# RMSNorm on one core: gamma on GpSimd's own queue, one early single-row store for three, and the last tile stored whole

## The chip, the cores and the metric

One core of a Trainium2 chip. The metric is the device time of one execution in microseconds (us); lower is better. The granted TensorE clock was 1.00, and TensorE has two instructions here, so the clock plays no part.

## The reference

```python
# x: 16 x 1024 x 512 float32, gamma: 512 float32 (all ones)
rms = np.sqrt(np.mean(x ** 2, axis=-1, keepdims=True) + 1e-5)
return (x / rms * gamma).astype(np.float32)
```

Input and output are 33.55 MB each, and nothing is reused between rows: 67.1 MB have to pass the DMA engines once.

## The kernel before

The 16384 rows are cut in 4 tiles of 128 partitions x 32 rows. Three slots of SBUF hold a tile each; tile 3 comes into slot 0 after tile 0 has been stored from it. A group is 16 rows of a tile (7 and 9 at the start). ScalarE squares, VectorE (DVE) sums, ScalarE takes the root and VectorE the reciprocal. Then GpSimd (POOL) takes `share` rows of the group through both multiplications; ScalarE scales the others one by one, and VectorE multiplies them by gamma in one instruction. All transfers are issued by SyncE (SP) in the order of the program.

```python
    pieces = (0, 128, 224, 320, 416, D)
    load(0, 0, 0, 1)                       # tile, slot, first row, end row
    load(0, 0, 1, 8)
    for c0, c1 in zip(pieces, pieces[1:]):
        nc.sync.dma_start(out=gamma_row[:, c0:c1], in_=gamma.unsqueeze(0)[:, c0:c1])
    load(0, 0, 8, 16)
    load(0, 0, 16, 32)
    load(1, 1, 0, 16)
    # ... ones_col, matmul gamma_psum = ones x gamma_row, later gamma_b = copy of gamma_psum
    groups = [                             # tile, first row, rows, pieces to square, GpSimd's share
        (0, 0, 7, (7,), 3), (0, 7, 9, (9,), 5), (0, 16, 16, (7, 9), 7),
        # ... (all with share 7)
        (3, 16, 16, (7, 5, 4), 3),
    ]
    # ...
    def transfers(t, g):                   # after the group's last instruction is written
        if (t, g) == (0, 0):
            store(0, 0, 0, 1)
            load(1, 1, 16, 32)
            store(0, 0, 1, 2)
            load(2, 2, 0, 23)
        elif (t, g) == (0, 16):
            store(0, 0, 2, 3)
            load(2, 2, 23, 32)             # these rows are scratch of the squares until then
            store(0, 0, 3, 16)
            store(0, 0, 16, 32)
            load(3, 0, 0, 16)
            load(3, 0, 16, 32)
        elif (t, g) == (1, 16):
            store(1, 1, 0, 32)
        elif (t, g) == (2, 16):
            store(2, 2, 0, 32)
        elif (t, g) == (3, 0):
            store(3, 0, 0, 16)
        elif (t, g) == (3, 16):
            store(3, 0, 16, 32)
    # ... for every group, with the squares of the next one in between:
        scale_by_pool(rstd, t, g, n, share)
        scale(rstd, t, g, 0, half)
        scale(rstd, t, g, half, mine)
        times_gamma(t, g, 0, mine)
        transfers(t, g)
```

## Time and profile before

| | before |
|---|---|
| median of the first three runs | 161.52 us (161.37 to 161.54) |
| the profiled execution | 161.95 us, span 160.2 us |
| DVE, ACT, POOL busy | 112.0, 107.8, 106.4 us |
| DMA share, first packet of x to last packet | 1.00 over 157.25 us |
| bytes moved | 67.12 MB in 2747 packets |

The prediction shows the lines that carry the bound. What the change moves at the start is seen in the timeline of SyncE's queue (start, us, issuer, line, transfer, count), kernel before:

```profile
0.74 0.86 SPq L45 DMA_DIRECT2D slot<-in_x_dram  x2
1.65 1.48 SPq L58 DMA_DIRECT2D gamma_row<-in_gamma_dram  x5
3.17 5.39 SPq L45 DMA_DIRECT2D slot<-in_x_dram  x3
27.35 0.35 SPq L49 DMA_DIRECT2D out_dram<-slot  x1
27.74 0.43 SPq L45 DMA_DIRECT2D slot<-in_x_dram  x1
28.27 0.38 SPq L49 DMA_DIRECT2D out_dram<-slot  x1
```

The times are those of the issue and not of the transfer: the single-row store issued at 27.35 ran at about 32, behind the 12.6 MB of loads issued before it.

### The profile page before, as it was taken

To read this page: it belongs to the slowest core of one execution; us is meant where nothing else is said; L and a number is where in the kernel's file an instruction comes from. 1 tells how busy PE (TensorE), PEld (TensorE's weight loads), DVE (VectorE), ACT (ScalarE), POOL (GpSimd) and SP (SyncE) were. 2 spreads that over 40 slices of the span, in tenths; PEclk is the share of its full clock that TensorE was granted. 3 is DMA by queue.
4 is the path that set the end of the run, shared out by engine and by line. 5 is a ranking of instruction groups with operands and counts; after the bars stand their busy time and mean duration, and the time that the engine had idled before them with its cause. 6 is when DMAs were issued, how large, how long until landed. Compare 5 with 4: busy or idle time off the path is not lost.

```text
span 160.2 us, 276 instructions
## 1 busy us (share of the span) xinstructions
PE 2.0 (1%) x2; PEld 0.5 (0%) x2; DVE 112.0 (70%) x39; ACT 107.8 (67%) x108; POOL 106.4 (66%) x24
## 2 busy tenths in 40 slices
PE   0050000000000000000000000000000000000000
PEld 0010000000000000000000000000000000000000
DVE  0018098899798999999999999999999009700000
ACT  3071967976999998999899899989960990000000
POOL 1000951994999599999999999999999980000000
DMA  5999999899999899999999999996996996999994
GB/s 189 431 421 475 442 401 458 340 446 491 417 435 494 388 379 383 426 450 475 434 401 426 483 401 393 524 491 295 524 491 295 524 491 295 401 491 417 401 450 196
DMA packets 2747, 67.12 MB, mean 419 GB/s; under 512 B 313, under 2 KB 314, under 8 KB 826
## 3 DMA queue, kind: packets, MB, share of 16 engines
q1 hardware_dynamic: 2746, 67.11, 98.1%
q14 instruction: 1, 0.01, 0.0%
HBM read 33.56 MB, written 33.55 MB: 419 GB/s over the span
## 4 chain that ended last, share of the span: by engine, by line
DVE 59%; ACT 22%; DMA 4%; ACTq 0%; issue 0%; SPq 0%
DVE ss L97 36%; DVE slot L122 23%; ACT slot L118 8%; ACT slot L96 7%; ACT sq_psum L96 6%; DMA slot<-in_x_dram 4%; DVE ss L103 1%; ACT ss L102 1%; ACTq L208 0%; ACT gamma_b L165 0%; SPq L45 0%; ACTq L96 0%
## 5 line engine op out<-in xcount | busy, mean ns | idle before, releaser
L109 POOL TENSOR_TENSOR slot<-slot,ss 128x3584 f32<-128x3584 f32 (+2 forms) x9 | 47.0, 5218 | 24.1 <-DVE ss L103 24.1
L110 POOL TENSOR_TENSOR slot<-slot,gamma_b 128x3584 f32<-128x3584 f32 (+2 forms) x9 | 59.3, 6587 | 0.7
L97 DVE TENSOR_REDUCE ss<-sq_psum 128x7 f32<-128x3584 f32 (+1 forms) x13 | 42.2, 3247 | 13.7 <-ACT sq_psum L96 13.7
L118 ACT ACTIVATE slot<-slot,ss 128x512 f32<-128x512 f32 x75 | 47.3, 706 | 4.7 <-DVE ss L103 4.7
L122 DVE TENSOR_TENSOR slot<-slot,gamma_psum 128x4608 f32<-128x4608 f32 (+2 forms) x9 | 41.3, 4590 | 8.7 <-ACT slot L118 8.7
L96 ACT ACTIVATE sq_psum<-slot 128x3584 f32<-128x3584 f32 (+1 forms) x13 | 34.6, 2658 | 6.4 <-DMA slot<-in_x_dram 5.7
L97 DVE TENSOR_REDUCE ss<-slot 128x9 f32<-128x4608 f32 x3 | 14.9, 4954 | 4.4 <-ACT slot L96 4.2
L97 DVE TENSOR_REDUCE ss<-sq_sbuf 128x5 f32<-128x2560 f32 x5 | 14.0, 2803 | 0.0
L96 ACT ACTIVATE slot<-slot 128x4608 f32<-128x4608 f32 x3 | 12.1, 4033 | 0.0
L96 ACT ACTIVATE sq_sbuf<-slot 128x2560 f32<-128x2560 f32 x5 | 11.6, 2321 | 0.0
L102 ACT ACTIVATE ss<-ss,eps_t 128x16 f32<-128x16 f32 (+2 forms) x9 | 2.7, 305 | 11.9 <-DVE ss L97 11.9
L103 DVE RECIPROCAL ss<-ss 128x16 f32<-128x16 f32 (+2 forms) x9 | 2.1, 236 | 0.4 <-ACT ss L102 0.4
L66 PE MATMUL gamma_psum<-gamma_row,ones_col 1*128 1x512 f32 x2 | 2.0, 1122 | 8.6 <-DMA gamma_row<-in_gamma_dram 8.6
L72 ACT ACT_TABLE_LOAD x1 | 1.3, 1283 | 1.2 <-PEq L197 1.2
L165 ACT COPY gamma_b<-gamma_psum 128x512 f32<-128x512 f32 x1 | 0.6, 567 | 0.0
L66 PEld LDWEIGHTS gamma_psum<-gamma_row,ones_col 1*128 1x128 f32 x2 | 0.5, 308 | 8.6 <-issue 8.6
L64 POOL MEMSET ones_col<- 1x128 f32 x1 | 0.2, 195 | 0.3 <-POOLq L197 0.3
L197 POOL MEMSET const-float32-0.0<- 128x1 f32 x1 | 0.1, 99 | 0.2 <-issue 0.2
L72 ACT ACTIVATE table<-eps_t 128x1 f32<-128x1 f32 x1 | 0.2, 202 | 0.0
L197 POOL MEMSET const-bfloat16-1.0<- 128x1 bf16 x1 | 0.1, 102 | 0.0
L197 POOL MEMSET const-uint8-127<- 128x1 uint8 x1 | 0.1, 102 | 0.0
L197 POOL MEMSET const-float32-1.0<- 128x1 f32 x1 | 0.1, 99 | 0.0
(1 smaller groups left out, 0.1 us busy)
## 6 DMA issues: line engine op xcount, KB each, us to landing
slot<-in_x_dram SPq DMA_DIRECT2D x5, 4096.0 KB, 21.9
out_dram<-slot SPq DMA_DIRECT2D x3, 4096.0 KB, 23.4
slot<-in_x_dram SPq DMA_DIRECT2D x1, 5888.0 KB
out_dram<-slot SPq DMA_DIRECT2D x1, 3328.0 KB, 21.8
slot<-in_x_dram SPq DMA_DIRECT2D x1, 2304.0 KB, 14.3
slot<-in_x_dram SPq DMA_DIRECT2D x1, 2048.0 KB, 9.9
slot<-in_x_dram SPq DMA_DIRECT2D x1, 1792.0 KB, 7.0
out_dram<-slot SPq DMA_DIRECT2D x3, 256.0 KB
```

The lines of the kernel that those rows point to most:

```text
L66: nc.tensor.matmul(gamma_psum[:, 0], ones_col, gamma_row, start=True, stop=True)
L72: nc.scalar.activation(out=table, in_=eps_t, func=AF.Sqrt)
L96: nc.scalar.activation(out=sq[:, :m], in_=rows, func=AF.Square)
L97: nc.vector.tensor_reduce(out=ss[:, r : r + m, 0], in_=sq[:, :m], axis=mybir.AxisListType.X, op=OP.add)
L102: nc.scalar.activation(out=ss[:, :n, 0], in_=ss[:, :n, 0], func=AF.Sqrt, bias=eps_t, scale=1.0 / D)
L103: nc.vector.reciprocal(out=ss[:, :n, 0], in_=ss[:, :n, 0])
L109: nc.gpsimd.tensor_tensor(out=part, in0=part, in1=by_row, op=OP.mult)
L110: last = nc.gpsimd.tensor_tensor(out=part, in0=part, in1=gamma_b.to_broadcast([P, share, D]), op=OP.mult)
L118: nc.scalar.activation(out=x[:, g + r, :], in_=x[:, g + r, :], func=AF.Copy, scale=rstd[:, r])
L122: scaled = nc.vector.tensor_tensor(out=part, in0=part, in1=gamma_psum.to_broadcast([P, r1 - r0, D]), op=OP.mult)
L165: nc.scalar.copy(out=gamma_b[:, 0], in_=gamma_psum[:, 0])
L197: nc = _bacc.Bacc("TRN2", target_bir_lowering=False, num_devices=1)
```

## The change

The intent is fewer transfers: gamma as one transfer on another queue, two single-row stores fewer, and one store for tile 3 in place of two. Since the last store then waits for the last group, the compute of that group is shortened: GpSimd takes 5 rows for 3, and VectorE starts after the first half of the scaling.

```diff
-    for c0, c1 in zip(pieces, pieces[1:]):
-        nc.sync.dma_start(out=gamma_row[:, c0:c1], in_=gamma.unsqueeze(0)[:, c0:c1])
+    nc.gpsimd.dma_start(out=gamma_row, in_=gamma.unsqueeze(0))
...
-        (3, 16, 16, (7, 5, 4), 3),
+        (3, 16, 16, (7, 5, 4), 5),
...
             load(1, 1, 16, 32)
-            store(0, 0, 1, 2)
             load(2, 2, 0, 23)
         elif (t, g) == (0, 16):
-            store(0, 0, 2, 3)
             load(2, 2, 23, 32)
-            store(0, 0, 3, 16)
+            store(0, 0, 1, 16)
...
-        elif (t, g) == (3, 0):
-            store(3, 0, 0, 16)
         elif (t, g) == (3, 16):
-            store(3, 0, 16, 32)
+            store(3, 0, 0, 32)
...
         scale(rstd, t, g, 0, half)
+        if not ahead:
+            times_gamma(t, g, 0, half)
...
-        times_gamma(t, g, 0, mine)
+        times_gamma(t, g, 0 if ahead else half, mine)
```

More of the change, by code (lines that the diff above doesn't have):

```diff
@@ L52 @@
     gamma_row = const.tile([1, D], fp32)
-    pieces = (0, 128, 224, 320, 416, D)
     load(0, 0, 0, 1)
     load(0, 0, 1, 8)
-    for c0, c1 in zip(pieces, pieces[1:]):
-        nc.sync.dma_start(out=gamma_row[:, c0:c1], in_=gamma.unsqueeze(0)[:, c0:c1])
+    nc.gpsimd.dma_start(out=gamma_row, in_=gamma.unsqueeze(0))
     load(0, 0, 8, 16)
```

## The prediction

> **What bounds the kernel now.** I began with the page's busy shares and the strips of 40 slices. No compute engine is over 70%, but the DMA strip is at 9 nearly from end to end:
>
> ```profile
> PE 2.0 (1%) x2; PEld 0.5 (0%) x2; DVE 112.0 (70%) x39; ACT 107.8 (67%) x108; POOL 106.4 (66%) x24
> ...
> DMA  5999999899999899999999999996996996999994
> ...
> DMA packets 2747, 67.12 MB, mean 419 GB/s; under 512 B 313, under 2 KB 314, under 8 KB 826
> ```
>
> The 6s near the end look like holes, so I asked the windows view for three stretches: before the first data packet, the stream, and after its last packet. I chose the borders from the packet records of the trace (first packet of x at 1.75 us, last one ends at 158.99). The columns are the stretch, its length, five engines' busy time, the granted clock, the DMA share and GB/s:
>
> ```profile
> 0.00:1.75 1.75, 0.00 (x0) 0.00 (x0) 0.00 (x0) 0.60 (x1) 0.44 (x6) 1.00 0.02 1
> 1.75:159.00 157.25, 2.04 (x2) 0.50 (x2) 112.05 (x39) 107.25 (x108) 106.00 (x18) 1.00 1.00 427
> 159.00:160.17 1.17, 0.00 (x0) 0.00 (x0) 0.00 (x0) 0.00 (x0) 0.00 (x0) 1.00 0.00 0
> ```
>
> The share is 1.00 over the whole 157.25 us, and this settles it: the 16 DMA engines never wait for work. The 6s come from counting long packets in the slice in which they start (one 64 KB packet takes 2.42 us in the records, more than half a slice). The span is 1.75 us of start, 157.25 us of transfer and 1.17 us of end.
>
> The chain that ended last gives DVE 59% and the DMA 4%, which would say that DVE is the bound. Its last piece shows what it leaves out: it follows instructions, and the last instruction ends at 139.14 us, 21 us before the span does.
>
> ```profile
> 132.05 7.09 DVE slot L122
> ```
>
> What follows that piece is seen in the SyncE queue's waits, where L208 is the end of the program (us in total, times, longest), and in the timeline of the last group:
>
> ```profile
> SPq L208 <- DMA out_dram<-slot: 19.6, 3, 9.6
> ```
>
> ```profile
> 123.95 8.07 ACT L118 ACTIVATE slot<-slot,ss 128x512 f32<-128x512 f32 x13 [4.72 <-DVE ss L103]
> 125.56 2.75 POOL L109 TENSOR_TENSOR slot<-slot,ss 128x1536 f32<-128x1536 f32 x1
> 125.62 13.91 SPq L49 DMA_DIRECT2D out_dram<-slot  x2
> 128.38 3.43 POOL L110 TENSOR_TENSOR slot<-slot,gamma_b 128x1536 f32<-128x1536 f32 x1
> 132.05 7.09 DVE L122 TENSOR_TENSOR slot<-slot,gamma_psum 128x6656 f32<-128x6656 f32 x1 [8.13 <-ACT slot L118]
> ```
>
> The first half of tile 3 is issued for storing at 125.62 and the second at about 139.2. By the packet records tile 2's store holds the engines until 138.7 (the first engine free) to 139.6 (the last), the first half of tile 3 until about 149, the second until 158.99. The second half was thus issued nearly 10 us before an engine could start on it. Compute ends early enough, and its time is hidden.
>
> **What the Trainium skill says.** "DMA: Bandwidth & Descriptors", section "Where 436 GB/s comes from", gives 435.2 GB/s as the ceiling of the ports. The trace agrees: 427 GB/s on average, 437 between 102 and 138 us (a window that rounds at packets), and 27.1 bytes per ns in a 64 KB packet, times 16 engines 434. So there is no unused bandwidth, beyond some 2 us of small and slow packets. The same page, "Issuing engines are not separate DMA queues", says that transfers issued by SyncE, ScalarE or GpSimd run on the same 16 engines, and that another issuer saves issue time only. The kernel before issues all from one queue (q1) and can't test it; the change can. "Why a DMA increments its semaphore by 16 and not by 1" says that one increment comes from each engine that a transfer uses. The trace agrees: 19 large transfers x 16, plus five gamma pieces with one data packet and one increment each, of which four have data under 512 B, are 304 + 5 + 4 = 313, the page's count under 512 B. "Latency and other measured facts" puts the first byte at about 0.6 us for SyncE's path and about 1 us for GpSimd's. Here the first load is issued at 0.74 (0.38 us of issue) and its packets start at 1.75; GpSimd's path is in no run yet.
>
> **The change part by part.**
>
> *Gamma.* Five issues (1.48 us of SyncE's time from 1.65 us on) leave SyncE's queue, so the next load is issued some 1.5 us sooner. That buys nothing: it was issued at 3.17, and its first packets run at 7.2, behind the 2 MB ahead of it. The five packets take 22 to 27 ns, with their increments about 0.16 us, on whichever engine holds them. On GpSimd's queue the built program cuts the row in 16 pieces of 128 B: one small packet and one increment on each engine, about 0.03 us each. The matmul that waits for gamma (8.6 us) should go sooner, but its first readers are the copy of gamma at 15.63 and GpSimd's multiply at 18.87. GpSimd's two memsets get later by the time of one issue; ScalarE is idle until 8.31 for x, so this is hidden. Worth: 0 to -0.15 us.
>
> *Early stores.* Rows 1 and 2 of tile 0 lose their own stores and go with the 13-row one, which becomes 15 rows. Bytes are equal, packets fewer: two transfers x 8 packets on each engine. A 2 KB packet takes 84 ns, where 27.1 bytes per ns would make 75.6: about 8 ns are fixed. The large ones agree: two 32 KB packets (1213 ns each) against one of 64 KB (2418) differ by 8 ns. So 16 x 8.4 = -0.13 us, and two increments of 9 ns, -0.02. The loads of tiles 1 and 2 come 0.7 to 1.4 us sooner in the queue, and the first rows' store later; nobody waits for either. The load of rows 23 to 31 of tile 2 still waits for DVE until 49.8, while the queue has work until about 56 (57.3 before, less two single-row stores of 0.7).
>
> *Tile 3 whole.* 8 packets and one increment fewer on each engine: -0.07 and -0.01 us. The store now waits for the last group. GpSimd takes 5 rows in place of 3: from 125.56 on, by the 5-row instructions already in this kernel (4.46 and 5.61 us, with gaps 10.14), it ends at 135.7. ScalarE scales 11 rows at 8.07 / 13 = 0.62 us: six are done at 127.7, all at 130.8. DVE multiplies them in two goes, at 0.54 us a row plus 0.1 (from 9 rows in 4.94 and 13 in 7.09): 6 rows to 131.0, 5 rows to 133.8. So GpSimd is last, the store is issued at 135.75, and with the 1.0 us that the first load needed its packets can run from 136.8. The first engine is free at 138.7 less the 0.2 saved so far: 138.5. Margin 1.7 us, so no hole.
>
> *Sum:* -0.13 - 0.02 - 0.07 - 0.01 - (0 to 0.15) = -0.23 to -0.38 us of 157.25. I take -0.3: 161.52 - 0.3 = 161.2.
>
> **Rivals.**
>
> *Compute was the bound after all.* The chain's shares speak for it, and the last instruction ends 3.4 us sooner (139.14 to 135.7): the time would be 158.1, just over 2% faster. The DMA share of 1.00 speaks against it.
>
> *The queue runs dry before the last store.* Tile 3's first half no longer fills the time while the last group is computed. If GpSimd or DVE ended 3 us later than I reckon, near 139 as before, the packets would start at 140.2: a hole of some 1.7 us, and 162.9. The durations of these instructions repeat to within 1% through the trace (seven-row multiplies 7.78 to 7.81), so I give it little. It is why the change moves two rows to GpSimd and splits DVE's work: without these two the whole store would lose time.
>
> *Slow packets.* Against the usual duration of their size, packets lose about 1.4 us per engine in all, in four places: the first 4 us, and the ends of the loads at 29 to 31, 61.5 to 62.5 and 99 us, each with a long run of stores (or the first row's) next in the queue. These three switches stay; the two that go (at 42 and 57 us) show no loss. So I expect no gain, but this is the widest uncertainty: half a microsecond either way.
>
> *GpSimd's queue costs something at start or end*, such as preparing descriptors before the first instruction, or one more queue to close. No view of before shows it. It could add 0.3 to 1 us outside the stream.
>
> **Range and chances.** The argument rests on the stream's 1.00 share, so all terms are tenths of a microsecond, and 2% is 3.2 us. The three runs of before lie within 0.17 us. Slow packets and the new queue set the range: 160.6 to 161.9. Faster by over 2% needs the first rival, slower needs the second twice as bad as reckoned: 2% each.
>
> **What would show it.** DMA share 1.00 from the first packet to the last; about 2340 packets (14 x 128 large, 2 x 128 of 2 KB, 16 x 16 increments, 32 for gamma) with the same bytes; GpSimd's last instruction ending at 135.7, DVE's near 133.8; the last store issued just after; the waiting at the program's end some 24 us on one store. The chain of waits should end 3.4 us earlier with the span hardly changed. I am wrong if the share dips between 135 and 141 us, if the stream starts later than 1.8 us, if the end takes more than 1.2 us after the last packet, or if packets of one size take other times than before.

## The result, and the profile after

Changed: median 161.51 us (161.43 to 161.68, 6 runs). Before, in the same rounds: 161.46 us (161.33 to 161.54, 6 runs). Ratio 1.0005, 95% interval 0.9992 to 1.0018, so the same. A ratio here is the mean time of one kernel's runs over that of the other's of the same rounds, so not quite the ratio of the medians. Executions over 1.5% slower than the fastest of the same kernel are left out of the means. 161.51 lies in the range of 160.6 to 161.9, but the forecast gain of 0.3 us isn't there: 0.3 us would be a ratio of 0.998, outside the interval.

The page of the changed kernel, the DMA strip, the packets, the queues and the shares of the chain that ended last:

```profile
DMA  6999999899998899999999999996996997999974
...
DMA packets 2337, 67.12 MB, mean 420 GB/s; under 512 B 288, under 2 KB 288, under 8 KB 544
...
q1 hardware_dynamic: 2304, 67.11, 98.1%
...
q0 software_dynamic: 32, 0.00, 0.0%
...
POOL 46%; ACT 18%; DVE 12%; DMA 4%; POOLq 4%; issue 0%; SPq 0%; ACTq 0%
```

The packets are those reckoned (2337, predicted about 2340), and gamma is on a queue of its own with 32. The chain has turned from DVE (59%) to POOL (46%) without any effect on the time: it names whichever engine ended its instructions last, and the DMA ends some 23 us after it. SyncE's waiting for stores at the program's end is 22.5 us in two waits, the longest 19.3, where some 24 us on one store were predicted.

The windows view of the changed kernel (stretch, length, five engines, clock, DMA share, GB/s), cut at its own last packet:

```profile
0.00:1.75 1.75, 0.00 (x0) 0.00 (x0) 0.00 (x0) 0.60 (x1) 0.73 (x5) 1.00 0.00 0
1.75:158.50 156.75, 2.04 (x2) 0.49 (x2) 111.05 (x40) 106.01 (x106) 110.25 (x21) 1.00 1.00 428
158.50:159.70 1.20, 0.00 (x0) 0.00 (x0) 0.00 (x0) 0.00 (x0) 0.00 (x0) 1.00 0.00 0
```

The start is the same, the end a little longer (1.24 us after the last packet at 158.47, 1.17 before; more than 1.2 was one of the prediction's signs of being wrong), and the share is 1.00 again. The stream is 0.5 us shorter than in the trace of before (156.75 for 157.25). On two traces alone one would say that the change saved 0.5 us. The timed runs deny it, because the profiled execution of before was a long one; the first experiment shows this.

The last group in the timeline of the changed kernel, engine by engine:

```profile
123.89 6.85 ACT L116 ACTIVATE slot<-slot,ss 128x512 f32<-128x512 f32 x11 [4.72 <-DVE ss L101]
...
125.47 4.47 POOL L107 TENSOR_TENSOR slot<-slot,ss 128x2560 f32<-128x2560 f32 x1
130.02 5.61 POOL L108 TENSOR_TENSOR slot<-slot,gamma_b 128x2560 f32<-128x2560 f32 x1
...
127.71 6.08 DVE L120 TENSOR_TENSOR slot<-slot,gamma_psum 128x3072 f32<-128x3072 f32 x2 [3.85 <-ACT slot L116]
...
135.65 0.33 SPq L49 DMA_DIRECT2D out_dram<-slot  x1
```

GpSimd ends at 135.63 (predicted 135.7), VectorE at 133.79 (133.8), the store is issued at 135.65 (135.75). By the packet records the first engine is free for it at 138.63 (138.5).

Gamma, from the timeline of GpSimd and the waits (in all, times, longest) of the changed kernel:

```profile
1.22 0.67 POOL L56 DMA_DIRECT2D gamma_row<-in_gamma_dram  x1 [0.78 <-POOLq L193]
```

```profile
PE gamma_psum L64 <- DMA gamma_row<-in_gamma_dram: 7.2, 1, 7.2
```

The matmul goes at 7.2 in place of 8.6 us and nobody gains by it: its readers come at 15.6 and 18.8. It is only 1.4 us sooner because gamma's packets first run at 5.47, 4.3 us after the issue began.

### The profile page after: what moved, and what is told of

The parts are those of the page before. It is cut to its first block, busy times and chain, and to the rows that moved or that the text cites. A ratio compares the mean times of both kernels' runs of the same rounds, so it can differ in the third digit from the quotient of the medians.

```text
span 159.7 us, 264 instructions
## 1 busy us (share of the span) xinstructions
PE 2.0 (1%) x2; PEld 0.5 (0%) x2; DVE 111.0 (70%) x40; ACT 106.6 (67%) x106; POOL 111.0 (69%) x25
## 2 busy tenths in 40 slices
DMA packets 2337, 67.12 MB, mean 420 GB/s; under 512 B 288, under 2 KB 288, under 8 KB 544
## 4 chain that ended last, share of the span: by engine, by line
POOL 46%; ACT 18%; DVE 12%; DMA 4%; POOLq 4%; issue 0%; SPq 0%; ACTq 0%
POOL slot L108 24%; POOL slot L107 22%; DVE ss L95 9%; ACT slot L94 7%; ACT sq_psum L94 6%; DMA slot<-in_x_dram 4%; POOLq L204 4%; ACT slot L116 3%; DVE slot L120 3%; ACT ss L100 1%; ACT gamma_b L159 0%; SPq L45 0%; DVE ss L101 0%; POOLq L107 0%; ACTq L94 0%
## 5 line engine op out<-in xcount | busy, mean ns | idle before, releaser
L107 POOL TENSOR_TENSOR slot<-slot,ss 128x3584 f32<-128x3584 f32 (+2 forms) x9 | 48.7, 5407 | 22.9 <-DVE ss L101 22.9
L108 POOL TENSOR_TENSOR slot<-slot,gamma_b 128x3584 f32<-128x3584 f32 (+2 forms) x9 | 61.5, 6828 | 0.7
L116 ACT ACTIVATE slot<-slot,ss 128x512 f32<-128x512 f32 x73 | 46.0, 706 | 4.7 <-DVE ss L101 4.7
L120 DVE TENSOR_TENSOR slot<-slot,gamma_psum 128x4608 f32<-128x4608 f32 (+3 forms) x10 | 40.3, 4040 | 4.4 <-ACT slot L116 4.4
L56 POOL DMA_DIRECT2D gamma_row<-in_gamma_dram x1 | 0.7, 667 | 0.8 <-POOLq L193 0.8
```

The source lines that it names most:

```text
L56: nc.gpsimd.dma_start(out=gamma_row, in_=gamma.unsqueeze(0))
L107: nc.gpsimd.tensor_tensor(out=part, in0=part, in1=by_row, op=OP.mult)
L108: last = nc.gpsimd.tensor_tensor(out=part, in0=part, in1=gamma_b.to_broadcast([P, share, D]), op=OP.mult)
L116: nc.scalar.activation(out=x[:, g + r, :], in_=x[:, g + r, :], func=AF.Copy, scale=rstd[:, r])
L120: scaled = nc.vector.tensor_tensor(out=part, in0=part, in1=gamma_psum.to_broadcast([P, r1 - r0, D]), op=OP.mult)
```

## The experiments

The runs were made in four batches, each on one chip with the kernel before beside it. "Slow packets" is worked out from the packet records: the duration of each packet over the usual one of its size (1213 ns for 32 KB, 686 for 18 KB), where the excess is more than 15 ns, summed over a stretch and divided by 16 engines. "Landing" is the last store's completion: each transfer increments its semaphore once per engine, so the trace has 16 times for it, and I give the median and the last. "Tail" is the span less the last landing, and "waits" are the wait instructions with which SyncE, at the end of the program, still has to go through other semaphores at or after that landing. The median is of the timed runs; all columns from "slow packets" on are of the one execution that was profiled, whose own time stands beside the median and is up to 1.2 us longer.

| kernel | median us | profiled us | slow packets 28 to 32.5 us | 32.5 to 65 | 97 to 104 | landing, median | landing, last | SyncE's transfers | waits | tail |
|---|---|---|---|---|---|---|---|---|---|---|
| before, the first trace | 161.52 | 161.95 | 0.27 | 0.39 | 0.22 | 158.85 | 159.34 | 24 | 1 | 0.83 |
| before again | 161.56 | 161.48 | 0.25 | 0.26 | 0.07 | 158.65 | 158.87 | 24 | 1 | 0.83 |
| changed | 161.51 | 161.48 | 0.27 | 0.38 | 0.08 | 158.63 | 158.81 | 16 | 1 | 0.90 |
| changed again | 161.62 | 161.61 | 0.18 | 0.52 | 0.07 | 158.59 | 158.94 | 16 | 1 | 0.90 |
| gamma only | 161.95 | 163.17 | 0.36 | 0.25 | 0.09 | 158.67 | 160.20 | 19 | 6 | 1.20 |
| early stores only | 161.77 | 161.77 | 0.27 | 0.44 | 0.09 | 158.82 | 159.04 | 22 | 3 | 0.96 |
| tile 3 whole only | 162.07 | 162.29 | 0.41 | 0.22 | 0.31 | 158.91 | 159.62 | 23 | 2 | 0.89 |
| whole store, compute as before | 162.56 | 162.51 | 0.12 | 0.71 | 0.03 | 159.74 | 159.83 | 16 | 1 | 0.90 |
| 14 more transfers | 162.62 | 163.68 | 0.56 | 0.10 | 0.63 | 159.81 | 160.88 | 30 | 3 | 1.02 |
| 29 more transfers | 166.39 | 165.67 | 0.17 | 0.50 | 1.12 | 161.26 | 162.81 | 45 | 4 | 1.09 |
| gamma and early stores | 161.82 | 162.05 | 0.19 | 0.70 | 0.19 | 159.00 | 159.21 | 17 | 4 | 1.06 |
| no early store | 161.84 | 161.75 | 0.00 | 0.90 | 0.04 | 158.86 | 159.02 | 15 | 2 | 0.96 |
| rows between loads | 161.85 | 161.77 | 0.28 | 0.25 | 0.10 | 158.60 | 158.88 | 18 | 5 | 1.11 |
| rows before loads | 162.50 | 162.47 | 0.88 | 0.02 | 0.05 | 159.12 | 159.57 | 18 | 5 | 1.12 |

### The kernel before, against itself

No edit.

> The kernel before, against itself, as the floor of noise and for a second trace. The trace that the prediction was made from took 161.95 us, 0.43 more than the median of the timed runs (161.52), so its stream of 157.25 us may have been an outlier. If it was, this run's span is near 159.8 us in place of 160.2 and the DMA stream (first packet of x to last packet) near 156.8 us; then the change saved nothing in the stream. If the stream is 157.2 us again while the time is 161.5, the stream is not what the timed runs lose. Ratio 1.000 with an interval of about 0.001 either way.

Measured: 161.56 us (161.44 to 161.74, 4 runs), ratio 0.9993, interval 0.9973 to 1.0014. The profiled execution was an ordinary one, 161.48 us with a span of 159.7, and its last packet ended at 158.53 us: the stream is 156.8 us and the first trace was the outlier. So the changed kernel's stream (to 158.47) is 0.06 us shorter than an ordinary one of before, not 0.5, and in its second trace below (to 158.59) 0.06 longer. The first trace's last engine landed 0.49 us after the median one, here 0.22.

### Each part alone

Gamma only: the first edit of the diff. Early stores only: the third. Tile 3 whole only: the others, with the group's five rows and two goes.

> Only gamma goes to GpSimd's queue; the other two parts as before. By the prediction's sum: 0 to -0.15 us, ratio 0.999 to 1.000. By the rival that GpSimd's queue costs something at start or end: +0.2 to +0.4 us (ratio 1.001 to 1.003), as time outside the span or as a later first packet.

> Only rows 1 and 2 of tile 0 are stored with the other 13. By the prediction: -0.15 us, ratio 0.999, stream 0.15 us shorter, 2747 - 2x128 - 2x16 = 2459 packets. By the rival that slow packets decide: the time moves by up to 0.4 us in either direction with the slow packets at the ends of the loads, whatever the count.

> Only tile 3 is stored whole, with GpSimd's five rows and DVE's two goes. By the prediction: -0.08 us, ratio 0.9995, the last store issued at 135.7 us and no dip of the DMA share between 135 and 141 us. By the rival that the queue comes close to running dry: +0.2 us or more, with a gap in the packets near 139 us.

Measured, all beside 161.61 us (161.38 to 162.47, 11 runs) of before: gamma 161.95 us (161.79 to 163.17, 6 runs), ratio 1.0029 (1.0002 to 1.0055); stores 161.77 us (161.67 to 161.88, 4 runs), ratio 1.0006 (0.9985 to 1.0026), 2459 packets as reckoned; whole 162.07 us (161.56 to 163.63, 6 runs), ratio 1.0045 (1.0006 to 1.0083). None gains. Two are even longer, with one or two executions of over 163 us among their six.

The trace of gamma's run is of such an execution (163.17 us) and shows what one is. Windows view, first the kernel before again, then gamma only:

```profile
101.00:102.00 1.00, 0.00 (x0) 0.00 (x0) 1.00 (x1) 1.00 (x1) 1.00 (x1) 1.00 0.00 0
...
158.50:159.00 0.50, 0.00 (x0) 0.00 (x0) 0.00 (x0) 0.00 (x0) 0.00 (x0) 1.00 0.00 0
```

```profile
101.00:102.00 1.00, 0.00 (x0) 0.00 (x0) 1.00 (x1) 1.00 (x1) 1.00 (x1) 1.00 0.15 66
...
158.50:159.00 0.50, 0.00 (x0) 0.00 (x0) 0.00 (x0) 0.00 (x0) 0.00 (x0) 1.00 0.15 66
```

66 GB/s in half a microsecond is one packet of 32 KB: one engine of 16 starts its last packet when the others have ended. At 101 us (a whole microsecond, so one packet of 64 KB, at 101.85) it is late already, since its last load of tile 3 took 1.89 us for 1.21; fifteen engines landed the last store by 158.81, the sixteenth at 160.20. Other executions of this kernel were not so late, but even the shortest, 161.79, is 0.4 over the shortest of before (161.38). That part is in the tail, 1.20 us for 0.83. The program's last line in the view of one line's instructions, from the last landing to the barrier of the engines (engine, operation, count, shortest/median/longest ns, first and last start), before again and then gamma only:

```profile
L208 SPq EVENT_SEMAPHORE  x1: 28/28/28, 158.9 to 158.9; - x1
```

```profile
L206 SPq EVENT_SEMAPHORE  x6: 17/28/28, 160.2 to 160.5; - x6
```

Before it ends, SyncE waits for each semaphore in a fixed order, mostly two by one instruction, and each instruction takes 0.06 us though the semaphores have long been reached. Eight semaphores go round among SyncE's transfers, as the built programs show. With 24 transfers, or 16, the last store has the eighth, and one instruction is left when it lands; with 19 it has the third, and six are left. The tails of the table are, within 0.03 us, 0.77 + 0.06 x waits where gamma is on SyncE's queue, and 0.84 + 0.06 x waits where it is on GpSimd's. So the rival "GpSimd's queue costs something at start or end" holds, with 0.07 us for the queue itself, where 0.3 to 1 us was feared; the other 0.30 us of this run are the number of transfers, which a part of the change turns and the full change turns back to a multiple of eight. The same correction explains most of the stores' part (0.13 of 0.16 us by medians). Of the whole tile's 0.46 us, 0.06 is the tail. The profiled execution (162.29 us) has a late engine (fifteen landed by 159.08 us, the last at 159.62); that the two of over 163 us are of this kind too is likely but not shown, since neither was profiled.

### The whole store without the help of the compute

The changed kernel, with

```diff
-        (3, 16, 16, (7, 5, 4), 5),
+        (3, 16, 16, (7, 5, 4), 3),
...
-        if not ahead:
-            times_gamma(t, g, 0, half)
...
-        times_gamma(t, g, 0 if ahead else half, mine)
+        times_gamma(t, g, 0, mine)
```

> The change without its edits of the last group: GpSimd keeps 3 rows and DVE one multiply of 13, so the last instruction ends at 139.1 us and the whole tile's store is issued at 139.2. If the margin was reckoned right (1.0 us from issue to first packet, engines free from 138.3 to 139.2 us): packets from 140.2, a hole of 1 to 2 us, all engines done at 140.2 + 19.4 = 159.6, time 162.6 us, ratio 1.007. If issue to first packet takes less behind a running queue: about 161.7. If compute is hidden anyway: 161.5.

Measured: 162.56 us (162.51 to 162.62, 4 runs), 1.0 us over the 161.56 of before in its rounds and over the changed kernel. (Its ratio, 1.0033 with an interval of 0.9978 to 1.0088, is blurred by executions of before of up to 163.77 us.) Windows view, the changed kernel, then this one:

```profile
138.00:139.20 1.20, 0.00 (x0) 0.00 (x0) 0.00 (x0) 0.00 (x0) 0.00 (x0) 1.00 2.02 874
139.20:140.20 1.00, 0.00 (x0) 0.00 (x0) 0.00 (x0) 0.00 (x0) 0.00 (x0) 1.00 0.00 0
```

```profile
138.00:139.20 1.20, 0.00 (x0) 0.00 (x0) 1.03 (x1) 0.00 (x0) 0.00 (x0) 1.00 0.01 0
139.20:140.20 1.00, 0.00 (x0) 0.00 (x0) 0.00 (x0) 0.00 (x0) 0.00 (x0) 1.00 2.46 1049
```

A packet counts in the stretch in which it starts, so a share of 2.02 is one 2.4 us packet on each engine. In the changed kernel the last store's first packets start before 139.2, one behind the other's end; here none starts between 138.0 and 139.93, since VectorE (1.03 in the first stretch) still multiplies. The store was issued at 139.10, so issue to packet took 0.83 us. By the packet records the 16 engines stand idle here for 0.9 us each around 139 us. This settles the second rival: the hole exists when the edits of the last group are left out, it costs 1.0 us, and with them there is a margin (138.63 less 135.65 less 0.83) of 2.1 us, for which the prediction had 1.7.

### The cost of a packet, seven times and more

The changed kernel, with

```diff
-            store(0, 0, 1, 16)
+            for r in range(1, 16):
+                store(0, 0, r, r + 1)
```

and in a second one rows 16 to 31 in the same way.

> The changed kernel with rows 1 to 15 of tile 0 stored one by one: 14 more transfers, so that the packet term is seven times what the change removed, with the opposite sign. By the prediction's 8.4 ns a packet and 9 ns an increment: 14 x (8 x 8.4 + 9) = +1.07 us, 162.6 us, ratio 1.0066. If the fixed cost of a packet lies beside the other packets of its engine and costs nothing: 161.5.

> The same with rows 16 to 31 as well: 29 more transfers than the changed kernel has. By 8.4 and 9 ns: +2.2 us, 163.7 us, ratio 1.0136, and twice what the run with 14 gives. If the time is a threshold and not a sum per packet, or SyncE's issuing (0.34 us each) lets the queue run dry: well over +2.2, with a DMA share below 1.00 between 62 and 85 us. If packets cost nothing: 161.5.

Measured: with 14 more transfers 162.62 us (median of five runs, 162.56 to 163.68; a sixth of 165.05, at a clock of 1.00 like the others), 1.06 over the 161.56 of before in these rounds, where 1.07 over the changed kernel was expected; 0.12 of it is the longer tail (1.02 for 0.90), which leaves some 0.95. With 29 more, 166.39 us (165.67 to 166.72, 6 runs), 4.8 over, where 2.2 was expected. The page of the first and its windows at the single rows:

```profile
DMA packets 4353, 67.12 MB, mean 415 GB/s; under 512 B 512, under 2 KB 512, under 8 KB 2688
```

```profile
62.00:71.20 9.20, 0.00 (x0) 0.00 (x0) 9.20 (x4) 8.64 (x9) 9.20 (x2) 1.00 1.05 403
```

The engines are busy all through and move 403 GB/s, which is 25.2 bytes per ns on each of the 16. One 2 KB packet by itself has 24.4 (84 ns), one of 64 KB has 27.1. So a small packet goes through every 81 ns and not every 84, and the share of 1.05 says the same: the records of small packets overlap by some 5%. Of a packet's 8 ns only about 5 are a cost in series.

The packet records give the whole sum, per engine and against the changed kernel's first trace. I add up every packet's usual duration, the time in which records overlap (more than 16 at once), and the slow packets. With 14 more transfers: usual durations +1.10 us, just as reckoned; overlap takes back 0.49; slow packets add 0.73. With 29 more: +2.12, -1.02 and +1.41. So the packets themselves cost 0.61 and 1.10 us, in proportion to their number and a little over half of what the prediction's term says. That the time came out at the expected 162.6 is luck: slow packets and late engines filled the gap. (The trace with 14 more is of a long execution, 163.68 us, so how much slow packets add in one of 162.6 isn't shown.)

In the trace with 29 more the last landing is 4.0 us later than the changed kernel's: 2.6 us in the median engine, nearly all of it these two terms, and 1.4 us because the 16 engines land further apart. The queue doesn't run dry there, as the expectation had as a rival: the share stays at 1.03 or more from 62 to 104 us. Of the changes tested this is the only one that is slower by the 2% rule (ratio 1.027). Why slow packets doubled, to 2.7 us per engine for 1.3, I don't know.

### The full change again, gamma with the early stores, and no early store at all

The changed kernel unchanged; the kernel before with the first and third edit; and the changed kernel with

```diff
-            store(0, 0, 0, 1)
             load(1, 1, 16, 32)
...
-            store(0, 0, 1, 16)
+            store(0, 0, 0, 16)
```

> The changed kernel once more, on another chip than at first. By the sum of the prediction: ratio 0.998. By what the traces have shown since (the packets saved, but slow packets at the end of the longer run of loads take it back, and the slowest of 16 engines sets the end): ratio 1.000, last landing near 158.8 us, its median engine near 158.6.

> Gamma and the early stores changed, tile 3 in two stores as before. Alone, gamma measured 1.0029 and the stores 1.0006. If those belong to the parts: 1.0035 here, and the whole-tile store would have to give it back in the full change, with no mechanism for it. If they are single late engines that come and go between executions: near 1.000, with a floor of 161.4 us like the others.

> The changed kernel without the one early single-row store: rows 0 to 15 of tile 0 go together, so that tiles 0, 1 and 2 are read in one run. If each switch from loads to stores costs slow packets (0.27 us at 29 to 31 us in the changed kernel): -0.08 for the 8 packets and up to -0.27, ratio 0.998. If it is the length of a run of loads that makes slow packets: those at 29 to 31 go, those before the first store grow by as much, ratio 1.000. If the slow packets at 29 to 31 stay though no store is near, they are tied to neither.

Measured beside 161.61 us (161.45 to 163.61, 9 runs) of before: the full change 161.62 (161.50 to 161.86, 5 runs), ratio 0.9989 (0.9944 to 1.0034); gamma and stores 161.82 (161.75 to 162.05, 5 runs), ratio 1.0003 (0.9957 to 1.0048); no early store 161.84 (161.75 to 161.98, 5 runs), ratio 1.0003 (0.9952 to 1.0055). The intervals are wide by one execution of before of 163.61. By medians the full change equals before on a second chip. Gamma's part and the stores' part don't add up to 1.0035: together they have 17 transfers and a tail of 1.06.

The kernel without an early store has the fewest packets of all (2193) and isn't the fastest, also without the 0.06 us that its tail has over the full change's. Its slow packets at 28 to 32.5 us are gone, so they belong to the switch from loads to a store that stands there in all the others. Those before the next switch, at about 60 us, are the most of all: 0.90 us per engine. The number of switches fell and the loss stayed.

### The same packets in two places

The changed kernel with rows 1 and 2 stored alone again, in one between the loads, in the other ahead of them:

```diff
 # rows between loads                 # rows before loads
     store(0, 0, 0, 1)                     store(0, 0, 0, 1)
                                     +     store(0, 0, 1, 2)
                                     +     store(0, 0, 2, 3)
     load(1, 1, 16, 32)                    load(1, 1, 16, 32)
+    store(0, 0, 1, 2)
     load(2, 2, 0, 23)                     load(2, 2, 0, 23)
+    store(0, 0, 2, 3)
     ...                                   ...
+    store(0, 0, 3, 16)              +     store(0, 0, 3, 16)
```

> The changed kernel with the single-row stores of rows 1 and 2 put back between the loads, where the kernel before has them. Theory: they part the long run of loads, and loads lose less to slow packets: between 32.5 and 65 us 0.2 to 0.4 us per engine, as in the four traces with these stores (0.39, 0.26, 0.25, 0.22), not 0.4 to 0.7 as in the five without (0.38, 0.52, 0.44, 0.70, 0.71). With 0.15 for the packets the median engine's last landing is at 158.5 to 158.6 us and the time 161.4 to 161.6. Rival, that slow packets come by chance whatever the order: 0.4 or more, and the time 161.7.

> The same transfers as in the run beside it, but rows 1 and 2 are stored right after row 0, before the loads: equal packets, and the long run of loads is whole again. Theory: slow packets between 32.5 and 65 us of 0.4 to 0.7 us per engine, so 0.2 to 0.3 us longer than the run beside it, 161.7 to 161.8. Rival, packets alone count: the same time as the run beside it, within 0.1 us.

Measured beside 161.57 us (161.40 to 162.36, 11 runs) of before: between the loads 161.85 us (161.67 to 163.75, 6 runs), four of them 161.67 to 161.94 and two late ones of 163.29 and 163.75, ratio 1.0044 (1.0003 to 1.0085); before the loads 162.50 us (162.47 to 162.95, 5 runs), ratio 1.0061 (1.0041 to 1.0082). Both have 2625 packets, and the second takes some 0.7 us more than the undisturbed runs of the first, with the same tail. Windows view around the first early stores, rows between loads, then rows before loads:

```profile
28.00:33.00 5.00, 0.00 (x0) 0.00 (x0) 4.43 (x2) 5.00 (x4) 4.92 (x2) 1.00 1.04 419
```

```profile
28.00:33.00 5.00, 0.00 (x0) 0.00 (x0) 4.48 (x2) 5.00 (x4) 4.92 (x2) 1.00 0.91 312
```

Part of the gap is that small packets stand in this stretch; the rest is loads that took up to 2.0 us for 1.2. So the rival that packets alone count falls. My theory got the direction right, the size too small (0.2 to 0.3 us expected, some 0.7 measured) and the place wrong: the slow packets of the second run are not at the end of the long run of loads (0.02) but before the three rows (0.88). With no, one and three single-row stores behind the first loads, these lost 0.00, 0.1 to 0.6 and 0.88 us. What decides how much the loads ahead of a store lose remains open.

## Why the prediction was right, and which term was not

**The bound.** Right. The share is 1.00 from first to last packet in the changed kernel as in before. By the packet records an engine stands idle for less than 0.1 us between 3 and 158 us in every trace but one. Every result above but that one can be read as a length of the DMA stream and the tail behind it, while GpSimd's busy time grew from 106.4 to 111.0 us without effect. The exception is the whole store without the help of the compute, where the stream has a hole.

**The first rival, compute as the bound.** Wrong, as reckoned: the last instruction ended 3.5 us sooner (135.63 for 139.14) and the time stayed.

**Tile 3 whole.** Right in each step: ends of the engines, issue, margin; the missing edits cost 1.0 us, where the rival said a hole of 1.7 (issue to packet was 0.83 us for 1.0, and the first engine was free at 138.89 for 138.5).

**Gamma.** Right that earlier arrival is worth nothing. The gain of up to 0.15 us isn't there: the usual durations of all packets add up to 155.67 us per engine with gamma alone changed and to 155.66 before. The rival's cost at the end is there: 0.07 us for the queue.

**Packets.** The count and the durations were right, but the term takes each packet's 8 ns as time in series, and about 3 of them overlap with the next packet: 0.61 us for 1.07 reckoned with 14 more transfers. For the change the usual durations fall by 0.21 us per engine, from 155.66 to 155.45 (0.23 reckoned), and 0.09 us less overlaps, so 0.12 is left. That is well under what an execution varies by.

**The sum, -0.3 us.** This is the step that failed, by about 0.3 us; the range of 160.6 to 161.9 held because it is four times as wide as the effect is large. Four things went into it. The prediction took the first trace as an ordinary execution, though its own time stood 0.43 us over the median; the second trace of before shows a stream of 156.8 us to start from. The packets were worth 0.12 us and not 0.23 to 0.38. Slow packets had half a microsecond either way in the range and nothing in the sum: over the whole execution they came to 1.10 us per engine in the second trace of before and to 1.28 and 1.33 in the two of the changed kernel, about 0.2 us more. But the first trace of before had 1.37, so two traces of one kernel differ by more than that, and a loss from the change isn't shown. Last, the sum has no term for the end of the program, though a rival names it, where the tail grew by 0.07. With -0.12, +0.2 and +0.07 against the second trace of before the sum is some 0.15 us, and the changed kernel's traces are 0.0 and 0.1 us longer than it, the timed medians 0.05 and 0.01. The traces agree on the stream: the median engine's landing at 158.65 before, 158.63 and 158.59 changed. It isn't shown that the merged stores cause slow packets. The four traces with single rows between the loads and the one made to test it have 0.22 to 0.39 us at 32.5 to 65 us, and the six of the changed kernel's order or nearest to it (changed, changed again, stores only, gamma and stores, compute as before, no early store) 0.38 to 0.90. But the run with 14 more single-row stores, which has no row between the loads either, had only 0.10, and the rows ahead of the loads moved the loss to another place.

**What the prediction did not think of.** The end is set by the slowest of 16 engines. Two executions that are over 0.7 us longer than their kernel's median were profiled: in gamma's one engine was 1.4 us later than the other fifteen, and in the one with 14 more single rows the 16 landings lie 1.4 us apart, where the changed kernel's lie 0.5 apart. I counted such executions after the fact: 11 of 70 in the kernels with single-row stores between the loads (before 6 of 52), none of 34 in those without and none of 6 with 29 more single rows, but 2 of 6 in the run with 14 more. So merging the early stores may have made the time steadier rather than shorter. It was not a planned test, and one could be planned: some 50 executions each.

No version that I ran beat both kernels. The rows between the loads with 16 or 24 transfers, and thus a tail 0.2 us shorter, would by this sum come to 161.5, where both kernels are; I did not run it.

## What to carry to other kernels

When the DMA share is 1.00 from the first packet to the last, the chain of waits and the busy shares of the engines explain nothing but whether the stream gets a hole: work out when the last store is issued, add the measured time from issue to first packet, and compare with when the queue before it is empty. Removing packets saves the part of their fixed time that doesn't overlap (here about 5 of 8 ns each on every engine), which is a reason to merge hundreds of them and none to merge a dozen. Before a difference of a few tenths of a microsecond is read from two traces, compare each profiled execution's own time with the median of the timed runs. And an edit that changes the number of transfers can move the end of the program by 0.06 us per wait instruction that is still to be gone through after the last transfer lands: a part of a change tested alone carries this along.

## What the Trainium skill lacked or had wrong

- "DMA: Bandwidth & Descriptors", "Latency and other measured facts": a first byte about 1 us after the issue on GpSimd's path. Here gamma was issued at 1.22 us (0.67 us of issue) and its first packet ran at 5.47, 4.3 us later, with all 16 engines busy with loads; it had landed 5.9 us after the issue. No run has this path with idle engines. On SyncE's path, where the page has 0.6, 1.0 us passed from the start of the issue to the first packet at the start, and 0.83 at the end with the engines idle; from the end of the issue it was 0.63 and 0.50. The page doesn't say from which point it counts, so on this path no disagreement is shown.
- The same page, "Specifications", has 512 B as the least transfer for line rate. Here 2 KB packets moved 25.2 bytes per ns on each engine and 64 KB packets 27.1, so 2 KB still lose 7%. That a packet has a fixed overhead the page says in a later section; only its size at 2 KB is new.
- No page I read has it that the loads ahead of a store slow down: 32 KB packets of up to 2.0 us in place of 1.21, 0 to 0.9 us per engine at one switch, in traces that differ in the order of the transfers.
- No page I read has the walk through the semaphores at the end of a program: 0.06 us for each wait instruction after the last landing, 1 to 6 of them here, so a tail of 0.83 to 1.20 us.
- No page I read tells how far one late engine of 16 can stretch a kernel that is alone on its core: in one trace fifteen engines landed the last store by 158.81 us and the sixteenth at 160.20. The records don't say which engine it was.
